# Row maxima of the prompt attention over 128 rows of q, and gate selection over 128 rows

## The chip, the cores and the metric

One core of a Trainium2 chip runs the whole kernel. The metric is device time in microseconds, the median of the runs of one kernel.

## What is computed

The reference is one step of a decoder layer, for a prompt of 512 positions and for 8 sequences of 4 new positions, with the same weights: a combined projection `h = x @ w_in`, four mixers (state space, short convolution, causal pooling, sparse attention), `w_out`, a layer norm, and a feed-forward part (`relu(x @ w_up)^2 @ w_down`) with another layer norm. All of it is in fp32. The change touches the attention of the prompt, of which this is the core:

```python
# selected and window branch; for 512 positions every block is selected, so both are causal softmax attention
s = jnp.einsum('bqgrd,bkgd->bgrqk', q, k).astype(f32) * (HEAD_DIM ** -0.5)
p = jax.nn.softmax(jnp.where(mask, s, NEG_INF), axis=-1)
o = jnp.einsum('bgrqk,bkgd->bqgrd', p, v)
...
gates = jax.nn.sigmoid(g_nsa).reshape(B, T, NSA_HEADS, 3)
y_d = gates[..., 0:1] * o_cmp + gates[..., 1:2] * o_sel + gates[..., 2:3] * o_win
```

There are 8 heads of 64 columns, in 2 groups g of 4 heads r, and 3 branches; the compressed branch works on 8 block averages instead of keys.

## The kernel before, in words

**Precision.** TensorE multiplies in a rounded form of fp32 (float32r). To keep precision, an operand is split into a high part (rounded) and a low part (the rest), and a product is made from three matmuls: high x high, high x low, low x high.

**The main stream.** The projections, `w_out`, `w_up` and `w_down` are a long row of such matmuls: weights of 128x128, activations of 272 columns (half of the 544 positions), into the accumulator `acc`. Weights come by DMA into `raw`; ScalarE makes the high part `wh`, VectorE or GpSimd the low part `wl`.

**Side work.** Everything else is written as Python generators (`gens`). The instruction order of each engine is fixed at build time: a small cost account (`Model`, one clock for each engine) is kept while instructions are written out, and between the matmuls of the main stream `step_side` lets one generator go on, if what it yielded is due: a tile that is ready by the account, a buffer that is free (`FREE_T`, `FREE_S`, `FREE_O`: the PSUM tiles t, s, o), an engine that is not too far behind (`lag`), or a flag. The account prices a float32r matmul by its columns alone unless one side has 32 rows or fewer; 64 and 128 rows cost the same in it. Each engine then runs its list in order, and waits on semaphores where an operand isn't there yet.

**The prompt attention** (`att_prompt`, line 1294) is such side work. There are 16 units u: 2 branches x 4 heads r x 2 groups g. `compressed(r)` makes the compressed branch for each r; `keys_values(br)` brings keys and values: `KH` holds the high part of the keys of g twice, in rows 0 to 63 and 64 to 127; `KL` has 65 rows, the low part of the keys and a row of -1.

**The maxima** (`maxima`, line 1396). For unit u, q is loaded twice into `qraw` (rows 0 to 63 and 64 to 127), and then `q2[:64]` is the high part of q (a copy on ScalarE), `q1` is the high part in all 128 rows (ScalarE), and in `q1[64:]` GpSimd puts the low part (a subtraction of 64x512). So `KH` x `q1`, over 128 rows, is keys-high times q-high plus q-low. The scores for the maxima are computed with the queries as weights, in three groups for each unit: query tiles 0 and 1 (128 and 256 key columns), 2 (384), 3 (512). VectorE masks the diagonal block and takes row maxima; they go by a transpose into row 64 of `q2`, so that the later score matmul (`KL` with `q2`, 65 rows) subtracts them. The maxima need not be exact, as they cancel. Up to NQ = 3 units may be ahead of the values.

**The scores and values.** For each unit and each of 4 key tiles: `KH` x `q1` (128 rows) and `KL` x `q2` (65 rows) into s, the exponential on ScalarE, its split into ph (ScalarE) and pl (GpSimd), three matmuls into o.

**The gates.** `g_done` (line 1276) keeps the sigmoids of the gates in `ghl`: high part in rows 0 to 23, low part in rows 32 to 55, zeros elsewhere. `gate_sel(br, r)` makes a matrix of zeros and ones from `gio`, an iota with the row number within 32 less 12 g: a matmul with it spreads the gate of one branch and head over the 128 rows of the output. It is used 12 times: four in `compressed`, right behind a matmul with the 16 rows of `Vcb`, and eight in `gated`, once for each pair of units.

The lines of the maxima before are 1424 (`yield FREE_T, q2, KL[br, g], ("lag", "V", LM)`) and 1428 (the matmul).

Of the kernel before, what the change touches and what calls it, by code (L numbers as in the profile page):

```python
# [25 lines left out]
F32R = mybir.dt.float32r  # L26
I32 = mybir.dt.int32
# [5 lines left out]
NP, NS, NB, TS = 512, 32, 8, 4  # L33
# [23 lines left out]
LV, LA, LM = 2.5, 2.0, 2.5  # L57
# [155 lines left out]
def tile_hybrid_trunk(ctx: ExitStack, tc: tile.TileContext, x_prompt, x_sample, cache_nsa_kv, cache_win_kv,  # L213
# [8 lines left out]
    V, A, G, PE, SP = (Engine(mdl, e, n) for e, n in ((nc.vector, "V"), (nc.scalar, "A"), (nc.gpsimd, "G"),  # L222
                                                     (nc.tensor, "T"), (nc.sync, "S")))
# [15 lines left out]
    def alloc(pool, tag, shape, dt=F32, bufs=1):  # L239
        t = pool.tile(list(shape), dt, tag=tag, name=nm(tag), bufs=bufs)  # L240
        mdl.alloc(t, tag, bufs)
        return t
# [4 lines left out]
    def ps(tag, shape=(128, 512), bufs=1):  # L247
        return alloc(pside, tag, shape, F32, bufs)

    def psS(shape=(128, 512)):  # L250
        return ps("s", shape, bufs=2)
# [8 lines left out]
    def spawn(gen):  # L260
        gens.append([gen, ()])
# [48 lines left out]
    FREE_T, FREE_O = ("free", "t", 1), ("free", "o", 1)  # L310

    def has(*names):
        return tuple(("flag", n) for n in names)
# [13 lines left out]
    def mm(out, lhsT, rhs, start=True, stop=True):  # L327
        PE.matmul(out, lhsT, rhs, start=start, stop=stop)
# [5 lines left out]
    def halves(t):  # L334
        return t.rearrange("p (h n) -> p h n", h=2)
# [306 lines left out]
    def tp(tag, shape, dt=F32, bufs=1):  # L642
        return alloc(mp, tag, shape, dt, bufs)
# [455 lines left out]
    def cp_tile(n):  # L1099
        return tp("cp", (128, 680), bufs=3)[:, :n]  # L1100
# [105 lines left out]
    KTn = tp("ktn", (128, 2, NS))  # L1206
    Vn = tp("vn", (NS, 2, 128))
    gtok = tp("gtok", (NS, 24))
    ghl = tp("ghl", (64, NP), F32R)
    Kcb, Vcb = tp("kcb", (128, 2, 8)), tp("vcb", (16, 128))  # L1210
    dpool = ctx.enter_context(tc.tile_pool(name="spill", bufs=1, space=bass.MemoryType.DRAM))
    qd = [dpool.tile([128, NP], F32, tag=f"qd{r}", name=nm("qd")) for r in range(4)]
# [63 lines left out]
    def g_done(acc):  # L1276
        gsg = cp_tile(NT)
        A.activation(halves(gsg[:24]), acc[:24, :, :HN], AF.Sigmoid)
        z0 = cp_tile(NP)
        V.memset(z0[:64], 0.0)  # L1280
        V.tensor_copy(ghl, z0[:64])
        A.copy(ghl[0:24, :], gsg[:24, :NP])
        V.tensor_sub(ghl[32:56, :], gsg[:24, :NP], ghl[0:24, :])
        spawn(g_gen(gsg))

    def g_gen(gsg):
        yield gsg, FREE_S
        t = psS()
        tr(t[:NS, :24], gsg[:24, NP:])
        A.copy(gtok, t[:NS, :24])  # L1290
        flags.add("g")


    def att_prompt():
# [4 lines left out]
        def t2(tag, shape, dt=F32, bufs=1):  # L1299
            return alloc(p2, tag, shape, dt, bufs)  # L1300
# [5 lines left out]
        V.tensor_scalar(cmask, ioc, 0.0, None, op0=OP.is_ge)  # L1306
        V.tensor_scalar(kneg, cmask, -1.0, -NEG, op0=OP.add, op1=OP.mult)

        gio = t2("gio", (64, 2, 64), I32)
        for hf in range(2):  # L1310
            G.iota(gio[hf * 32:hf * 32 + 32], pattern=[[-12, 2], [0, 64]], base=0, channel_multiplier=1)

        def gate_sel(br, r):
            gs = t2("gsel", (64, 2, 64), F32R, 2)
            V.tensor_scalar(gs, gio, float(3 * r + br), None, op0=OP.is_equal)
            return gs

# [4 lines left out]
        def compressed(r):  # L1322
# [29 lines left out]
            pT = t2("p", (128, NP))  # L1352
            A.copy(pT[:16], t[:16])
            gs_ = gate_sel(0, r)
            yield pT, gs_, FREE_SS
            op, gp = psS(), psS()
# [11 lines left out]
        KH, KL, VH, VL, Q, G_ = {}, {}, {}, {}, {}, {}  # L1368
# [27 lines left out]
        def maxima():  # L1396


            def load(u):
                r, g = divmod(u % 8, 2)  # L1400
                qr = t2("qraw", (128, NP), bufs=2)
                for dup in range(2):
                    SP.dma_start(qr[dup * 64:dup * 64 + 64], qd[r][g * 64:g * 64 + 64])
                return qr

            nxt = load(0)
            for u in range(16):
                br, g = u // 8, u % 2
                qr = nxt
                if u >= NQ:  # L1410
                    yield has(("pv", u - NQ))
                yield qr,
                q1, q2 = t2("q1", (128, NP), F32R, NQ), t2("q2", (65, NP), F32R, NQ)
                A.copy(q2[:64], qr[:64])
                A.copy(q1, qr)
                G.tensor_sub(q1[64:], qr[64:], q1[64:])
                Q[u] = (q1, q2)
                if u + 1 < 16:
                    nxt = load(u + 1)
                if u % 8 < 2:  # L1420
                    yield has(("kp", br, g))
                mx = t2("mx", (128, 4), bufs=2)
                for qts in ((0, 1), (2,), (3,)):
                    yield FREE_T, q2, KL[br, g], ("lag", "V", LM)
                    s_, c = ps("t"), 0
                    for qt in qts:
                        n = (qt + 1) * 128
                        mm(s_[:, c:c + n], q2[:64, qt * 128:qt * 128 + 128], KH[br, g][:64, :n])
                        c += n
                    c = 0  # L1430
                    for qt in qts:
                        n = (qt + 1) * 128
                        V.tensor_add(s_[:, c + n - 128:c + n], s_[:, c + n - 128:c + n], mask_qk)
                        V.reduce_max(mx[:, qt:qt + 1], s_[:, c:c + n], axis=AX.X)
                        c += n
                yield mx, FREE_T
                mt = ps("t")
                for qt in range(4):
                    PE.transpose(mt[0:1, qt * 128:(qt + 1) * 128], mx[:, qt:qt + 1], ident)
                A.copy(q2[64:65, :], mt[0:1, :])  # L1440
                flags.add(("mx", u))
# [27 lines left out]
        def gated(i, rec, tmp):  # L1469
            br, r = divmod(i, 4)  # L1470
            gs_ = gate_sel(1 + br, r)
            for q in range(4):
                yield rec, LAG_V
                V.reciprocal(rec[:, q * 128:(q + 1) * 128], rec[:, q * 128:(q + 1) * 128])
            yield rec, gs_, FREE_S
            gp = psS()
            mm(gp, gs_.rearrange("p g d -> p (g d)"), ghl)
            V.tensor_mul(rec, rec, gp)
            V.tensor_mul(tmp, tmp, rec)
            V.tensor_add(yd[r][:, :NP], yd[r][:, :NP], tmp)  # L1480
            flags.add(("gated", i))

        yield ("at", mdl.clk["T"] + AT2),
        for r in range(4):
            spawn(compressed(r))
        spawn(keys_values(0))
        gens.insert(0, [maxima(), ()])
        todo = []
        for u in range(16):
            br, g = u // 8, u % 2  # L1490
# [3 lines left out]
            for kt in range(4):  # L1494
# [5 lines left out]
                q1, q2 = Q[u]  # L1500
                s_ = psS()
# [339 lines left out]
    acc = run_tile(U["g"], 0, 24, xr, ks16, True)  # L1841
    drain_side(("kv", KV_ORDER[-1]))
    g_done(acc)
    spawn(att_prompt())
    spawn(att_sample())
    gc_done(0, run_tile(U["gc", 0], 0, 128, xr, ks16, True))
# [424 lines left out]
```

## Time and profile before

| | |
|---|---|
| median of 3 runs | 2464.77 us (2460.89 to 2469.05) |
| profiled execution, its own time | 2462.9 us |
| its span, first to last instruction | 2461.1 us |
| TensorE busy | 2333.4 us, 95% |
| VectorE busy | 1521.9 us, 62% |
| ScalarE busy | 995.8 us, 40% |
| GpSimd busy | 843.9 us, 34% |
| HBM traffic | 107 GB/s over the span |

In the profile PE is TensorE's matmuls, PEld its loads of weights (which run beside matmuls), DVE VectorE, ACT ScalarE, POOL GpSimd and SP the engine that issues DMAs. A matmul counts as busy from its start to a modelled end, so consecutive matmuls overlap, and a busy TensorE may still be slower than it could be: the distance from one start to the next tells more. A row names its output and inputs by the program's tiles: `t<-kh,q` are the matmuls of the maxima, `s<-q,kh` and `s<-q,klm` the scores, `o<-...` the values, `s<-ghl,gsel` the gates, `acc<-...` the main stream. As a helper records every instruction, all have line 160, and one goes by the names.

### The profile page before, as it was taken

Reading aid. Unit: us, or ns where it says so; the run is one execution under the profiler, and the core shown is the slowest. Engines: PE = TensorE matmul, PEld = TensorE weight load, DVE = VectorE, ACT = ScalarE, POOL = GpSimd, SP = SyncE. Lnnn points to the kernel's source line nnn. Section 1 sums busy time; section 2 is a strip of 40 time slices with the busy share of each in tenths; the row PEclk is TensorE's granted clock in tenths of the full one; section 3 lists DMA queues with packets and bytes.
Section 4 is the critical chain, followed back from the end, with each engine's and each line's share of the span. In section 5 each row is a group of like instructions: output and inputs, shape, how many; then the busy total and the mean of one; then the engine's idle time right before and its main releaser. Section 6 shows DMA issues by size and latency. Waiting matters only on the chain. (4 is left out here: it accounts for less than half of the span.)

```text
span 2461.1 us, 46914 instructions
## 1 busy us (share of the span) xinstructions
PE 2333.4 (95%) x18659; PEld 2242.7 (91%) x18659; DVE 1521.9 (62%) x2707; ACT 995.8 (40%) x1941; POOL 843.9 (34%) x726
## 2 busy tenths in 40 slices
PE   7999999998898798999999999999999999999995
PEld 6999888988787687999999999999999999999985
DVE  6873435567544766335694694694694694694256
ACT  3543355554334555323333333333333333333353
POOL 2342245555426598200240240240240240240255
PEclk9999999999999888999999999999999999999998
DMA  6533322322559454422333333233233233233443
GB/s 175 138 91 92 109 69 61 87 66 61 147 154 239 125 138 117 141 86 87 86 90 101 85 90 102 84 90 103 83 91 103 83 90 103 82 91 106 134 155 108
DMA packets 425703, 260.81 MB, mean 106 GB/s; under 512 B 30143, under 2 KB 407067, under 8 KB 425412
## 3 DMA queue, kind: packets, MB, share of 16 engines
q1 hardware_dynamic: 425035, 256.88, 36.6%
q8 instruction: 147, 2.41, 0.4%
q0 software_dynamic: 448, 0.93, 0.2%
q14 instruction: 73, 0.59, 0.1%
HBM read 249.26 MB, written 12.85 MB: 107 GB/s over the span
## 5 line engine op out<-in xcount | busy, mean ns | idle before, releaser
L160 PE MATMUL acc<-B,wh 128*128 128x272 f32 (+1 forms) x3552 | 980.0, 291 | 6.9 <-ACT B L160 2.9
L160 ACT CAST wh<-raw 128x512 fp32r<-128x512 f32 x749 | 462.0, 620 | 826.8 <-PE acc L160 651.9
L160 PEld LDWEIGHTS acc<-B,wh 128*128 128x128 f32 (+1 forms) x3552 | 675.1, 190 | 16.0 <-issue 4.3
L160 PE MATMUL acc<-C,wh 128*128 128x272 f32 x2456 | 676.0, 292 | 13.3 <-DVE C L160 10.0
L160 DVE TENSOR_TENSOR wl<-raw,wh 128x512 fp32r<-128x512 f32 x473 | 407.5, 873 | 326.4 <-ACT wh L160 312.8
L160 PE MATMUL acc<-B,wl 128*128 128x272 f32 x2560 | 580.4, 292 | 0.4 <-POOL wl L160 0.4
L160 POOL TENSOR_TENSOR wl<-raw,wh 128x512 fp32r<-128x512 f32 x276 | 379.1, 1383 | 448.0 <-ACT wh L160 397.9
L160 PEld LDWEIGHTS acc<-C,wh 128*128 128x128 f32 x2456 | 465.7, 191 | 19.7 <-DVE C L160 15.5
L160 PEld LDWEIGHTS acc<-B,wl 128*128 128x128 f32 x2560 | 422.7, 190 | 6.6 <-issue 5.2
L160 PE MATMUL acc<-uh,wh 128*128 128x272 f32 (+2 forms) x1088 | 314.5, 293 | 13.5 <-DVE A L160 13.4
L160 PE MATMUL acc<-ul,wh 128*128 128x272 f32 (+2 forms) x1088 | 309.1, 288 | 0.3 <-DVE fv L160 0.3
L160 POOL TENSOR_TENSOR tt<-raw,raw 128x512 f32<-128x512 f32 x48 | 63.3, 1318 | 714.6 <-DVE S L160 345.2
L160 PE MATMUL acc<-uh,wl 128*128 128x272 f32 (+2 forms) x1088 | 294.4, 290 | 5.6 <-POOL wl L160 5.6
L160 PE MATMUL acc<-A,wh 128*128 128x272 f32 (+1 forms) x992 | 278.9, 299 | 1.2 <-ACT C L160 1.0
L160 PEld LDWEIGHTS acc<-uh,wh 128*128 128x128 f32 x1088 | 206.1, 189 | 21.6 <-issue 17.1
L160 PE MATMUL acc<-A,wl 128*128 128x272 f32 (+1 forms) x992 | 214.0, 297 | 0.6 <-DVE wl L160 0.6
L160 DVE TENSOR_TENSOR A<-A,acc 128x272 f32<-128x272 f32 (+3 forms) x283 | 139.0, 503 | 116.5 <-ACT A L160 79.4
L160 PEld LDWEIGHTS acc<-ul,wh 128*128 128x128 f32 x1088 | 206.5, 190 | 0.6 <-DVE fv L160 0.6
L160 PEld LDWEIGHTS acc<-uh,wl 128*128 128x128 f32 x1088 | 197.6, 189 | 6.9 <-POOL wl L160 6.9
L160 PEld LDWEIGHTS acc<-A,wh 128*128 128x128 f32 (+1 forms) x992 | 187.3, 189 | 8.6 <-issue 4.6
L160 DVE TENSOR_TENSOR wl<-tt,wh 128x512 fp32r<-128x512 f32 x192 | 189.6, 987 | 8.4 <-ACT wh L160 8.4
L160 ACT CAST wh<-tt 128x512 fp32r<-128x512 f32 x192 | 118.6, 621 | 184.3 <-PE acc L160 103.0
(537 smaller groups left out, 3672.4 us busy)
## 6 DMA issues: line engine op xcount, KB each, us to landing
raw<-in_w_up_dram SPq DMA_DIRECT2D x144, 512.0 KB
raw<-in_w_down_dram SPq DMA_DIRECT2D x144, 512.0 KB
raw<-in_w_in_dram SPq DMA_DIRECT2D x52, 512.0 KB
page<-in_cache_nsa_kv_dram SPq DMA_DIRECT2D x64, 256.0 KB
raw<-in_w_out_dram SPq DMA_DIRECT2D x23, 512.0 KB
raw<-in_w_out_dram SPq DMA_DIRECT2D x34, 256.0 KB
C<-in_x_prompt_dram SPq DMA_DIRECT2D x16, 256.0 KB
raw<-in_w_in_dram SPq DMA_DIRECT2D x16, 256.0 KB
```

The costliest lines, as they stand in the source:

```text
L160: r = f(*a, **k)
```

## The change

The matmuls of the maxima use `q1` (128 rows, high and low part of q) and all 128 rows of `KH`, in place of the 64 rows of `q2` and of `KH`; the generator yields `q1` in place of `q2`. For the gates, `ghl`, `gio` and the selection matrices have 128 rows in place of 64: the zeros are written over 128 rows, and the iota runs four times over 32 rows instead of twice. Rows 64 to 127 of `ghl` are zeros, so they add nothing.

```diff
-    ghl = tp("ghl", (64, NP), F32R)
+    ghl = tp("ghl", (128, NP), F32R)
...
-        V.memset(z0[:64], 0.0)
-        V.tensor_copy(ghl, z0[:64])
+        V.memset(z0, 0.0)
+        V.tensor_copy(ghl, z0)
...
-        gio = t2("gio", (64, 2, 64), I32)
-        for hf in range(2):
+        gio = t2("gio", (128, 2, 64), I32)
+        for hf in range(4):
             G.iota(gio[hf * 32:hf * 32 + 32], pattern=[[-12, 2], [0, 64]], base=0, channel_multiplier=1)

         def gate_sel(br, r):
-            gs = t2("gsel", (64, 2, 64), F32R, 2)
+            gs = t2("gsel", (128, 2, 64), F32R, 2)
...
-                    yield FREE_T, q2, KL[br, g], ("lag", "V", LM)
+                    yield FREE_T, q1, KL[br, g], ("lag", "V", LM)
                     s_, c = ps("t"), 0
                     for qt in qts:
                         n = (qt + 1) * 128
-                        mm(s_[:, c:c + n], q2[:64, qt * 128:qt * 128 + 128], KH[br, g][:64, :n])
+                        mm(s_[:, c:c + n], q1[:, qt * 128:qt * 128 + 128], KH[br, g][:, :n])
```

## Rows read from the trace of the kernel before

**Rows 1.** The page: busy us of each engine, share of the span, instructions.
```profile
PE 2333.4 (95%) x18659; PEld 2242.7 (91%) x18659; DVE 1521.9 (62%) x2707; ACT 995.8 (40%) x1941; POOL 843.9 (34%) x726
```

**Rows 2.** Busy time by stretches (columns: PE, PEld, DVE, ACT, POOL, clock, DMA share, GB/s).
```profile
320.00:360.00 40.00, 40.00 (x261) 33.41 (x260) 10.19 (x27) 18.77 (x38) 16.85 (x16) 1.00 0.22 60
...
1040.00:1080.00 40.00, 40.00 (x324) 40.00 (x323) 14.38 (x21) 8.27 (x14) 0.00 (x0) 1.00 0.30 100
```

**Rows 3.** Timeline of TensorE at 337 us: start, duration (us), what, [idle before].
```profile
337.23 0.40 PE L160 MATMUL s<-q,kh 128*128 128x512 f32 x1
337.47 0.39 PE L160 MATMUL s<-q,klm 65*128 65x512 f32 x1
337.70 0.41 PE L160 MATMUL acc<-A,wl 128*128 128x272 f32 x2
```

**Rows 4.** The same at 291 us, unit 1's first group (x2: two matmuls).
```profile
290.74 0.41 PE L160 MATMUL acc<-A,wl 128*128 128x272 f32 x2
291.08 0.49 PE L160 MATMUL t<-kh,q 64*128 64x128 f32 x2
291.50 0.40 PE L160 MATMUL acc<-A,wh 128*128 128x272 f32 x1
291.74 0.29 PE L160 MATMUL acc<-B,wh 128*128 128x272 f32 x1
```

**Rows 5.** The same at 312 us, unit 2's 512-column group.
```profile
311.80 0.29 PE L160 MATMUL acc<-E,wh 128*128 128x272 f32 x1
312.01 0.50 PE L160 MATMUL t<-kh,q 64*128 64x512 f32 x1
312.44 0.52 PE L160 MATMUL acc<-C,wl 128*128 128x272 f32 x2
312.80 0.29 PE L160 MATMUL acc<-A,wh 128*128 128x272 f32 x1
```

**Rows 6.** The same at 426 us, a gate matmul (one acc matmul left out).
```profile
426.16 0.42 PE L160 MATMUL acc<-A,wl 128*128 128x272 f32 x2
426.51 0.50 PE L160 MATMUL s<-ghl,gsel 64*128 64x512 f32 x1
...
427.17 0.29 PE L160 MATMUL acc<-B,wh 128*128 128x272 f32 x1
```

**Rows 7.** The same at 344 us, scores of 128 columns (two rows left out).
```profile
344.01 0.41 PE L160 MATMUL acc<-A,wl 128*128 128x272 f32 x2
344.26 0.22 PE L160 MATMUL s<-q,kh 128*128 128x128 f32 x1
...
344.61 0.29 PE L160 MATMUL acc<-B,wh 128*128 128x272 f32 x1
```

**Rows 8.** Groups of GpSimd, 252 to 640 us: count | busy us, mean ns.
```profile
L160 POOL TENSOR_TENSOR wl<-raw,wh 128x512 fp32r<-128x512 f32 x70 | 93.9, 1344 | 80.4 <-ACT wh L160 68.7 <-PE acc L160 10.2 <-ACT cp L160 1.0
...
L160 POOL IOTA gio<- 32x128 int32 x2 | 0.5, 228 | 0.1
```

**Rows 9.** Weight loads beside kh: ns min/median/max, first and last start (us).
```profile
L160 PEld LDWEIGHTS t<-kh,q x64: 182/183/334, 280.6 to 563.8; 64*128 64x128 f32 x64
...
L160 PEld LDWEIGHTS s<-q,kh x64: 186/188/330, 337.1 to 621.9; 128*128 128x128 f32 x64
```

**Rows 10.** Timeline of GpSimd, unit 1: the subtraction into q1.
```profile
291.56 1.29 POOL L160 TENSOR_TENSOR q<-qraw,q 64x512 fp32r<-64x512 f32 x1 [0.56 <-POOL wl L160]
```

**Rows 11.** Waits of TensorE, 252 to 640 us: total us, times, longest (seven left out).
```profile
PE acc L160 <- DVE C L160: 4.0, 4, 2.0
...
PE s L160 <- ACT p L160: 0.5, 1, 0.5
```

**Rows 12.** Waits of TensorE, 640 to 1000 us, the longest in total.
```profile
PE s L160 <- DMA page<-in_cache_nsa_kv_dram: 10.7, 13, 2.8
```

**Rows 13.** Busy time by stretches around a fall of the clock (columns as in rows 2).
```profile
393.20:403.50 10.30, 9.47 (x34) 7.87 (x33) 8.17 (x14) 2.48 (x6) 4.69 (x4) 0.50 0.29 78
403.50:413.50 10.00, 10.00 (x73) 9.27 (x73) 4.24 (x11) 6.17 (x14) 4.79 (x5) 1.00 0.09 25
```

**Rows 14.** Timeline of TensorE: the last gate matmul of the prompt attention.
```profile
633.93 0.49 PE L160 MATMUL s<-ghl,gsel 64*128 64x512 f32 x1
```

## What the change does to the time: the prediction

> **What bounds the kernel now.** I read the totals first: TensorE is busy for 95% of the span [rows 1]. So the question for any edit is what it does to TensorE's stream. Next I read the busy table by stretches and compared the stretch in which the prompt attention runs as side work (its maxima and gates lie from 280.6 to 633.9 us [rows 9, 14]) with a stretch of the dense part [rows 2]. Both show TensorE busy for 40.00 of 40 us at full clock, yet the first holds 261 matmuls and the second 324. A matmul of 272 columns comes every 0.1235 us in the dense stretch; some of what counts as busy in the attention is therefore time in which TensorE finishes something and feeds nothing. The third view, the timeline of TensorE, shows where that time lies.
>
> The scale is 0.125 us for a 272-column matmul (so 0.46 ns per column); two side matmuls of 512 columns, one with 128 rows and one with 65, follow each other and the stream in 0.47 us, 0.235 each, which is the same scale with nothing over [rows 3].
>
> A group of the maxima with **64 rows** is different. From 290.74 to 291.74 the stream holds two 272-column matmuls, the group's 128 and 256 columns, and one more 272: 3 x 0.125 + 384 x 0.00046 = 0.55 us of columns in 1.00 us. So 0.45 us is lost, part ahead of the group and part behind it: after the matmul at 291.50, the first full-height one, the next starts 0.24 later and not 0.125 [rows 4]. The 512-column group: one 272, the group, two 272 are 0.375 + 0.235 = 0.61 us, and they take from 311.80 to 312.80, so 0.39 us is lost, and no row of it names a wait [rows 5]. The gate matmul (64 rows, 512 columns): two 272, itself and one 272 are 0.61 us and take from 426.16 to 427.17, so 0.40 us is lost [rows 6]. As 65 rows lose nothing and 64 rows lose 0.4 us at the same size, between the same neighbours, I put the loss down to the height of at most 64 rows: at a change between that height and the full one the array seems to be emptied, and the next weights not to be loaded ahead.
>
> Two pages of the Trainium skill pull apart here. "TensorEngine Tiling (Array Packing)", Tiling Modes (Key Properties), says that changing the tiling mode, not only the tile, drains TensorE; it gives no price, and the rows put 0.39 to 0.45 us on one round trip. "TensorE: Matmul & The Clock Gate", in its part on LDWEIGHTS, says that time goes by the columns and that the row count doesn't matter; taken alone it leaves nothing to gain, which is rival (a).
>
> **The change, part by part.** Maxima: 16 units of three groups each (columns 128+256, 384, 512), 64 matmuls. Their row count becomes 128, so they should cost what the 128-row score matmuls beside them cost. Lost today per unit: 0.45 + 0.39 + 0.39 = 1.23 us (for 384 columns I take the value of 512, the nearest row). Left afterwards: nothing for 384 and 512 [rows 3]; for the short one of 128 columns, two such in a row take the stretch from 344.01 to 344.61, which holds three 272 and two 128, 0.375 + 0.118 = 0.49 us, so 0.11 for two and 0.05 for one [rows 7]. Saving 1.23 - 0.06 = 1.17 us per unit, 16 x 1.17 = **18.7 us**. The low bound is half of that, 9 us, if only one of the two sides of a round trip goes; the high bound is 16 x 1.23 = 19.7 us. A loss from streaming itself I exclude, since the same weights and sizes at full height lose nothing [rows 3].
>
> Gates: eight gate matmuls of the two softmax branches stand between full-height matmuls: 8 x 0.40 = 3.2 us. The four of the compressed branch come right behind a matmul of 16 rows (Vcb), so one change of height stays in either case and I count half, 4 x 0.2 = 0.8 us, bounds 0 and 1.6. Together **4.0 us**.
>
> Added work: two more iotas on GpSimd, 2 x 0.23 us, once, before the attention starts [rows 8]; GpSimd is mostly idle there and nobody waits, so nothing; uncovered it would be 0.5 us. The wider memset, copy, and selection tiles have the same elements per partition and so, taken by the durations of before, the same time. The loads of weights take about the same in both heights, 183 and 188 ns in the median [rows 9].
>
> The moved wait: the first group of a unit now waits for all of q1, whose lower half GpSimd writes, and not for q2, which ScalarE writes. In unit 1 that subtraction runs from 291.56 to 292.85 us [rows 10], while the first group ran at 291.08 [rows 4]: 1.77 us too early for the new operand. Behind a waiting matmul on TensorE's queue stands the main stream. If the group kept its place, the price would be up to 16 x 1.77 = 28 us. But the place isn't fixed: the generator yields q1, and the planner emits the group only when its own account has q1 ready, so the group is put about 1.8 us later and main-stream matmuls fill the time. The nearest row is the value matmuls, whose third operand pl is also a GpSimd subtraction and is also waited for in this way: TensorE's list of waits in the attention has nothing of GpSimd among its nine rows [rows 11]. I take 0; bounds 0 and 28. The delay itself hides behind the lead that the maxima have over the scores (up to three units).
>
> Given back: TensorE already waits 13.8 us in this stretch, mostly for VectorE and ScalarE in few places (nine rows, 4.0 to 0.5 us) [rows 11]. A TensorE that is early reaches such a place early and waits longer, by what it saved since the last wait, about 1 us each at the two large places: 2 us. What comes after 640 us (the sample attention, which waits 10.7 us for its pages [rows 12]) starts when the prompt attention ends and shifts with it.
>
> **Sum**: 18.7 + 4.0 - 2 = 20.7 us. The profiled execution took 2462.9 us (its span is 2461.1, with 1.8 us around it), so 2442.2; the median of the runs shown lies 1.9 us above the profiled one, so I forecast **2444 us**.
>
> **Rivals.** (a) The number of rows doesn't matter: the 0.4 us belongs to the place (a write to another PSUM bank, a wait for the copy of q), and stays. Then about 2465. For it: weight loads last the same in both heights [rows 9]. Against: the 65-row matmuls, which also write another bank and also wait for q2 [rows 3]. The second page of the Trainium skill named above (TensorE: Matmul & The Clock Gate, on LDWEIGHTS) speaks for it; [rows 9] agree with it on the load's own duration, and [rows 3 to 5] don't for the stream.
>
> (b) Slower: GpSimd runs behind the planner's account, and the first group of each unit stops the main stream. Place: the subtraction into q1, behind splits of weights on GpSimd of 1.34 us each [rows 8]. The point from which it decides is 22.7 / 16 = 1.42 us of wait per unit; one split ahead eats the gain (16 x 1.34 = 21 us), two cost 16 x 2.69 = 43 us, 2464.8 + 43 - 22.7 = 2485. Against: [rows 11], where nothing waits for GpSimd.
>
> (c) Part is given back behind the attention, or by the new order: the planner's order shifts a little everywhere, and TensorE's clock falls after a pile of waits. A stretch of 10.3 us at half clock held 34 matmuls, the next 10 us at full clock 73 [rows 13]: one such stretch more costs 5 us, and later page loads several more. Two such things leave 8 to 12 us of gain: 2453 to 2460.
>
> (d) More: the stretch at half clock [rows 13] follows waits and contains 64-row groups. If it and the shorter ones go, 5 to 9 us come on top: 2435 and below, to about 2430.
>
> **How the numbers follow.** Forecast 0.66 (2436 to 2453); (a) 0.07; (b) 0.06; (c) 0.12, half of it a gain above the limit; (d) 0.09. Within 0.3%, about what a measurement of this kernel can tell from no change, means 2457.4 to 2472.2. Faster: 0.66 + 0.09 + 0.06 = 0.81; same: 0.07 + 0.06 = 0.13; slower 0.06. The range goes from 2431, into (d), to 2458, into (c); it leaves out (a), (b) and a part of (c) and (d).
>
> **What would show it.** In the profile of after: the maxima's matmuls with 128 rows, about 0.39 us and not 0.5 at 512 columns, and next to them the next stream matmul at its normal distance; more matmuls per 40 us between 280 and 635; the last gate matmul, in the trace of before at 633.93 us [rows 14], about 20 us earlier, and everything behind it shifted by about that much. Wrong step by step: if the distances stay, (a); if waits of TensorE for GpSimd's q1 show up, (b); if the attention ends 20 us earlier and the end of the kernel doesn't, (c).

## The result, and the profile after

| | before | after |
|---|---|---|
| median | 2464.61 us (6 runs, the three above among them) | 2448.33 us (2446.31 to 2451.93, 6 runs) |
| ratio | | 0.9938, 95% interval 0.9926 to 0.9949 |
| profiled execution, span | 2461.1 us | 2446.6 us |
| once more, beside later experiments | 2462.59 us | 2446.03 us, ratio 0.9929 (0.9916 to 0.9942) |

The change takes 16.3 us off the median, 16.6 in the comparison made later; 20.7 were forecast, and 2444 us.

The stretch of [rows 2] in the kernel after, and another of the attention, first before and then after (columns as there):

```profile
320.00:360.00 40.00, 40.00 (x274) 34.78 (x273) 13.31 (x41) 19.18 (x36) 19.14 (x18) 1.00 0.28 75
...
400.00:440.00 40.00, 40.00 (x276) 36.80 (x276) 19.11 (x40) 22.66 (x48) 21.08 (x20) 0.96 0.21 59
400.00:440.00 40.00, 39.92 (x300) 38.27 (x299) 23.12 (x45) 23.15 (x49) 22.75 (x21) 1.00 0.29 80
```

Busy as before, but with 274 matmuls where [rows 2] had 261, and 300 where there were 276 (at a granted clock of 0.96). The timeline of TensorE in the kernel after, for the three forms of [rows 4], [rows 5] and [rows 6]: a group of 128 and 256 columns, one of 512, and a gate.

```profile
357.23 0.29 PE L160 MATMUL acc<-B,wh 128*128 128x272 f32 x1
357.36 0.40 PE L160 MATMUL t<-kh,q 128*128 128x128 f32 x2
357.59 0.41 PE L160 MATMUL acc<-A,wl 128*128 128x272 f32 x2
357.84 0.29 PE L160 MATMUL acc<-A,wh 128*128 128x272 f32 x1
...
323.39 0.29 PE L160 MATMUL acc<-B,wh 128*128 128x272 f32 x1
323.52 0.40 PE L160 MATMUL t<-kh,q 128*128 128x512 f32 x1
323.75 0.41 PE L160 MATMUL acc<-A,wl 128*128 128x272 f32 x2
324.00 0.29 PE L160 MATMUL acc<-A,wh 128*128 128x272 f32 x1
...
413.27 0.41 PE L160 MATMUL acc<-A,wl 128*128 128x272 f32 x2
413.52 0.39 PE L160 MATMUL s<-ghl,gsel 128*128 128x512 f32 x1
413.75 0.29 PE L160 MATMUL acc<-A,wh 128*128 128x272 f32 x1
413.87 0.29 PE L160 MATMUL acc<-B,wh 128*128 128x272 f32 x1
```

The first stretch takes 0.61 us for 0.55 of columns, so 0.06 is lost where 0.45 was; the second 0.61 for 0.61 and the third 0.60 for 0.61, where 0.39 and 0.40 were lost. But not every group looks like this. The waits of TensorE's weight loads between 252 and 640 us (total us, times, longest), first of the kernel before, then of the kernel after, have one line that grew by much:

```profile
PEld t L160 <- DVE mx L160: 1.1, 1, 1.1
```

```profile
PEld t L160 <- DVE mx L160: 4.4, 10, 1.2
```

A group of the maxima waits in ten places for VectorE's row maximum of the group ahead of it, which reads the one PSUM tile t. One of them, on the timeline of weight loads after:

```profile
452.83 0.19 PEld L160 LDWEIGHTS t<-kh,q 128*128 128x128 f32 x1 [0.20 <-DVE mx L160]
```

The matmuls at this place, of which no row names a wait:

```profile
452.43 0.41 PE L160 MATMUL acc<-A,wl 128*128 128x272 f32 x2
452.83 0.50 PE L160 MATMUL t<-kh,q 128*128 128x512 f32 x1
453.17 0.29 PE L160 MATMUL acc<-A,wh 128*128 128x272 f32 x1
```

From 452.43 to 453.17 are 0.74 us for 0.485 of columns, so about 0.25 us of the 0.39 is still lost here.

Two more places matter. The last gate matmul, which stood at 633.93 [rows 14], and the pause of the main stream behind the loop over `op`, where it waits for the sample attention to end (TensorE's timeline; the last matmul of the stream ahead of the pause and the first behind it). Kernel before:

```profile
837.47 0.29 PE L160 MATMUL acc<-B,wl 128*128 128x272 f32 x1
...
867.09 0.60 PE L160 MATMUL acc<-B,wh 128*128 128x272 f32 x1 [0.26 <-ACT B L160]
```

Kernel after:

```profile
628.73 0.39 PE L160 MATMUL s<-ghl,gsel 128*128 128x512 f32 x1
...
814.75 0.37 PE L160 MATMUL acc<-B,wl 128*128 128x272 f32 x1
...
852.24 0.39 PE L160 MATMUL acc<-B,wh 128*128 128x272 f32 x1 [0.26 <-ACT B L160]
```

The stream reaches its pause 22.7 us earlier, 814.75 against 837.47, which is just the sum forecast for the rows, 18.7 and 4.0; but the prompt attention ends only 5.2 us earlier, and the pause lasts 37.5 us and not 29.6. From its end on everything is about as early, 14.9 us there and 14.5 at the end of the span.

### The profile page after: what moved, and what is told of

Its sections match the earlier page's. It is cut to its first block, busy times and chain, and to the rows that moved or that the text cites. A ratio compares the mean times of both kernels' runs of the same rounds, so it can differ in the third digit from the quotient of the medians.

```text
span 2446.6 us, 46935 instructions
## 1 busy us (share of the span) xinstructions
PE 2315.5 (95%) x18659; PEld 2243.8 (92%) x18659; DVE 1523.0 (62%) x2707; ACT 996.4 (41%) x1941; POOL 844.1 (35%) x728
## 5 line engine op out<-in xcount | busy, mean ns | idle before, releaser
L160 PEld LDWEIGHTS acc<-C,wh 128*128 128x128 f32 x2456 | 466.3, 191 | 20.9 <-DVE C L160 16.5
```

The lines of the kernel that those rows point to most:

```text
L160: r = f(*a, **k)
```

## The experiments

Four questions: is it the height of 64 rows; what does the new order do; what does the new wait cost; where are the missing microseconds. As the planner fixes the order of every engine by its account, an experiment can keep an order exactly by giving the account the operands that belong to it, while the engine gets others. Times stand beside those of the kernel before of the same comparison (2463.41, 2463.04 and 2462.59 us for the three sets).

**Order and height apart.** First the new order with the old 64 rows:

```diff
-                    yield FREE_T, q2, KL[br, g], ("lag", "V", LM)
+                    yield FREE_T, q1, KL[br, g], ("lag", "V", LM)
...
-                        mm(s_[:, c:c + n], q2[:64, qt * 128:qt * 128 + 128], KH[br, g][:64, :n])
+                        o_ = s_[:, c:c + n]
+                        nc.tensor.matmul(o_, q2[:64, qt * 128:qt * 128 + 128], KH[br, g][:64, :n], start=True, stop=True)
+                        PE.account("matmul", (o_, q1[:, qt * 128:qt * 128 + 128], KH[br, g][:, :n]), {})
```

> The instructions of before (64 rows everywhere) in exactly the order of after: the planner's account is told of q1, so the groups of the maxima are placed as in after, but the matmuls read q2 and 64 rows. My theory (each change between 64 rows and full height costs TensorE 0.4 us, 22.6 us in all, and the new order by itself costs several us because the prompt attention ends later in the main stream): some 20 to 23 us slower than after, 2468 to 2471 us, that is 3 to 7 us slower than before. Rival (the gain is the order's and rows don't matter): like after, 2448 us. Distances around a 64-row group in the trace by my theory: 0.39 to 0.45 us lost, as before.

Measured: 2463.58 us, ratio 1.0001 (0.9987 to 1.0014). So the order alone is worth nothing, and not the 3 to 7 us that I expected it to cost; against this kernel the rows of after are worth 15 to 18 us (medians of 2448.33 and 2446.03). The last gate (timeline of TensorE):

```profile
645.68 0.50 PE L160 MATMUL s<-ghl,gsel 64*128 64x512 f32 x1
```

It stands at 645.68 us, 11.8 later than in the kernel before: in the new order 126 more matmuls of the main stream (3478 against 3352), 15.7 us of them, come ahead of the prompt attention's end. This is why the attention of after ends only 5.2 us earlier. With the rows of after in the same order it moves from 645.68 to 628.73, by 17.0 us, and the end of the span by as much (2463.7 to 2446.6).

Two executions can differ by a few us through the granted clock alone. As an estimate, I count as lost half of the time for which a trace shows it at 0.50, the level of 1.2 GHz. Up to the last gate this is 12.0 us in new_order_64 and 12.0 in after, so the 17.0 us aren't the clock's; in the kernel before it is 10.2. The order of after with 128 rows was profiled twice more up to this point, in after_again and lead below: last gates at 628.33 and 626.50, with 12.0 and 10.2 us lost. Less these, all three stand within 0.5 us (616.3 to 616.8).

Then the old order with the new 128 rows (the same edit the other way round, `yield ... q2` and the account told of q2, the matmul on q1):

> The instructions of after (128 rows everywhere) in exactly the order of before: the account is told of q2, so a group of the maxima keeps its place, and TensorE really waits for GpSimd's half of q1. Theory: the stream gains 22.6 us, and the first group of 12 of the 16 units stands 0.6 to 1.8 us ahead of the end of that subtraction in the trace of before, 15 us of waits; 2455 to 2460 us, with waits for GpSimd's q in the list of TensorE. If the waits cost nothing: 2442. Rival (rows don't matter): 2465 or, with the waits, 2475 to 2480.

Measured: 2460.09 us, ratio 0.9988 (0.9977 to 0.9999), at the upper end of the 2455 to 2460 that the theory gave. The waits of TensorE from 252 to 640 us:

```profile
PE t L1430 <- POOL q L160: 14.0, 12, 1.7
```

Twelve waits for GpSimd's half of q1, 14.0 us, the longest 1.7: these are the places where [rows 10] stands behind [rows 4]. Had the planner left the groups where they were, most of the gain would have gone.

**The height by one row.** Row 64 of q2 gets a copy like the rows above it, and a second copy of the keys has a zero there, so that the result stays that of 64 rows; order of before, no wait for GpSimd:

```diff
-                A.copy(q2[:64], qr[:64])
+                A.copy(q2[:65], qr[:65])
...
+                nc.scalar.copy(kz[:64], kr[:64])
+                nc.vector.tensor_scalar(kz[64:65], neg1[64:65, :].to_broadcast([1, NP]), 0.0, None, op0=OP.mult)
...
-                        mm(s_[:, c:c + n], q2[:64, qt * 128:qt * 128 + 128], KH[br, g][:64, :n])
+                        nc.tensor.matmul(o_, q2[:65, qt * 128:qt * 128 + 128], KZ[br, g][:65, :n], start=True, stop=True)
```

> One row more: the maxima are those of before, but with 65 rows (row 64 of q2 holds a finite value, row 64 of a second copy of the keys is zero, so the result is that of 64 rows), in exactly the order of before and without any wait for GpSimd; four copies of 64x512 on ScalarE and four of one row on VectorE are added. Theory (what counts is whether more than 64 rows are used): 16 x 1.17 = 18.7 us of stream, all in the old order, so 2446 to 2449 us, though the maxima gain no precision and the gates stay at 64 rows. Rival (cost goes with the number of rows, or 128 of them are needed): 2464 us.

Measured: 2449.56 us, ratio 0.9937 (0.9924 to 0.9950). Its timeline of TensorE:

```profile
369.82 0.29 PE L160 MATMUL acc<-B,wh 128*128 128x272 f32 x1
369.95 0.40 PE L1432 MATMUL t<-kz,q 65*128 65x512 f32 x1
370.19 0.42 PE L160 MATMUL acc<-A,wl 128*128 128x272 f32 x2
370.44 0.29 PE L160 MATMUL acc<-A,wh 128*128 128x272 f32 x1
```

From 369.82 to 370.44 are 0.62 us for 0.61 of columns: one row more, and the 0.39 us of [rows 5] are gone. The height is the cause, and 65 rows do as well as 128. The time is 13.9 us less; 18.7 us of stream and 2446 to 2449 us had been expected. The last gate stands at 621.1 us, 12.8 earlier than before, though by the estimate above 3.4 us more were lost to the clock ahead of it (13.7 against 10.2), so some 16 us are won there at equal clock.

**The gates alone** (the lines of the diff on `ghl`, `z0`, `gio` and `gsel`):

> Only the gates have 128 rows; the order of TensorE is that of before. Theory: 8 x 0.40 + 4 x 0.2 = 4.0 us of stream, all of it ahead of the end of the prompt attention: 2460 to 2461 us, gate matmuls of about 0.39 us in place of 0.50. Rival (rows don't matter): 2464.6, no change in distances.

Measured: 2462.66 us, ratio 0.9992 (0.9983 to 1.0001): not told apart from no change. The distances are as expected; its timeline:

```profile
428.31 0.41 PE L160 MATMUL acc<-A,wl 128*128 128x272 f32 x2
428.56 0.40 PE L160 MATMUL s<-ghl,gsel 128*128 128x512 f32 x1
428.80 0.29 PE L160 MATMUL acc<-A,wh 128*128 128x272 f32 x1
```

0.49 us for 0.485, and eight such savings of 0.4 should show as 3 us. The profiled execution has a loss of this size ahead of the gates, in the stretches at the attention's beginning (columns as in [rows 2]), gates_only and then the kernel before:

```profile
272.60:282.60 10.00, 7.86 (x61) 7.35 (x60) 3.88 (x14) 3.40 (x6) 4.14 (x3) 1.00 0.72 218
282.60:292.60 10.00, 10.00 (x39) 8.73 (x40) 4.33 (x14) 1.14 (x2) 1.26 (x1) 0.50 0.20 53
```

```profile
272.60:282.60 10.00, 9.21 (x72) 8.63 (x71) 4.86 (x14) 3.41 (x6) 4.04 (x3) 1.00 0.78 244
282.60:292.60 10.00, 10.00 (x72) 8.87 (x73) 5.18 (x17) 4.08 (x8) 3.62 (x3) 1.00 0.39 118
```

In gates_only TensorE was idle for 2.1 of 10 us, and the granted clock of the next 10 us is 0.50, the level of 1.2 GHz, with 39 matmuls; before, 0.8 us idle, full clock, and 72 matmuls. From 252.6 to 302.6 us gates_only has 308 matmuls and the kernel before 340, though before's clock falls too in the last ten (0.83). Around the 12 gates the distances lose 3.9 us in all, where they lost 7.4 before, so 3.5 us are saved at the gates; but up to the last gate 13.7 us went to the lower clock, where it had been 10.2, and so this execution reaches it only 0.4 us earlier (633.5 us). In this execution the saving is there, and the clock hides it. Whether the timed runs lost their 3 us in the same way isn't settled.

Both parts without the moved wait (65 rows for the maxima, 128 for the gates, order of before):

> Both parts without the moved wait: maxima of 65 rows (as in rows65), gates of 128 rows, order of before. Theory: what rows65 gained (13.9 us) and the gates' 3.5 to 4 us: 2445 to 2447 us, level with after or up to 3 us faster. Rival (the gates' gain is lost again in waits, as gates_only alone showed only about 1 us): 2449.

Measured: 2446.83 us, ratio 0.9935 (0.9922 to 0.9949). Level with after, as expected; beside rows65 the gates' share is within the intervals.

**The missing microseconds.** In after the planner was made to leave the tile t free for 0.4 us before the next group:

```diff
+                elif x[0] == "free_m":
+                    if mdl.free_at(*x[1:3]) + x[3] > now:
+                        return False
...
-                    yield FREE_T, q1, KL[br, g], ("lag", "V", LM)
+                    yield ("free_m", "t", 1, 0.4), q1, KL[br, g], ("lag", "V", LM)
```

> After, and the planner emits a group of the maxima only when its account has had the PSUM tile t free for 0.4 us. Theory (in after TensorE waits ten times, 4.4 us in all, for VectorE's row maximum of the group ahead, which the emptying of the array used to cover): these waits go, 3 to 5 us less, 2443 to 2446 us; the order changes a little too, worth 2 us either way. Rival (the missing 4 us lie elsewhere): 2448.

Measured: 2458.01 us, ratio 0.9981 (0.9973 to 0.9990), some 10 us slower than after; the profiled execution was the fastest of the twelve, 2452.62 us. The test failed as a test: the order changed, and the waits of TensorE from 252 to 640 us are still there, with others beside them.

```profile
PE t L160 <- DVE mx L160: 3.7, 4, 2.0
PE t L160 <- POOL q L160: 3.4, 2, 1.8
```

So it says nothing on the price of the waits, and only that a new order can cost 10 us. The same margin on the 65-row kernel:

> rows65_gates with the same margin of 0.4 us. Theory: its waits of TensorE for the row maxima are already few (about 2 us), so 0 to 2 us faster than rows65_gates, 2443 to 2446 us; the order changes.

Measured: 2450.15 us, ratio 0.9946 (0.9932 to 0.9960), 3 us more than without it, which the intervals don't tell from nothing; it too says nothing on the price of the waits.

A cleaner way keeps the order of after and takes the work away that is waited for: the 64 additions of the mask ahead of the row maxima, which the account still counts. The maxima then run over the whole diagonal block; they only get larger, and cancel. The kernel after was run beside it.

```diff
-                        V.tensor_add(s_[:, c + n - 128:c + n], s_[:, c + n - 128:c + n], mask_qk)
+                        d_ = s_[:, c + n - 128:c + n]
+                        V.account("tensor_add", (d_, d_, mask_qk), {})
```

> The changed kernel once more, on the chip of the next three, so that they can be compared with it: 2446 to 2450 us.

> After, in exactly its order, without the 64 additions of the mask ahead of the row maxima (19 us of VectorE; the maxima then run over the whole diagonal block and are only larger, which cancels). The account still counts them. Theory (in after the groups of the maxima wait ten times for VectorE, 4.4 us, seven of these 0.2 to 0.26 us, less than the 0.3 us that goes per group): most of these waits go and TensorE gains 3 to 4 us: 2444 to 2446 us, with under 2 us of waits for mx left. Rival (these waits aren't what is missing): level with after.

Measured: 2446.03 us for after and 2444.26 without the additions, ratios 0.9929 (0.9916 to 0.9942) and 0.9922 (0.9910 to 0.9935). Waits of the weight loads from 252 to 640 us and the last gate, first after, then without the additions:

```profile
PEld t L160 <- DVE mx L160: 3.2, 9, 0.9
...
628.33 0.39 PE L160 MATMUL s<-ghl,gsel 128*128 128x512 f32 x1
```

```profile
PEld t L160 <- DVE mx L160: 0.4, 1, 0.4
...
622.22 0.39 PE L160 MATMUL s<-ghl,gsel 128*128 128x512 f32 x1
```

Eight of the nine waits are gone, and the attention ends 6.1 us earlier, in the same order: that is more than the waits themselves (3.2 us), as VectorE has 19 us less to do in this stretch. Of these 6.1 us the median shows 1.8, which the intervals don't tell from nothing.

What is lost at the groups can be added up from the timelines: from the start of the matmul ahead of a group to the start of the second one behind it, less 0.46 ns for each column between. Over the 48 groups of the maxima this is 20.2 us in new_order_64, 5.5 in after, 4.2 in after's second execution and 1.3 without the additions; over the 12 gates it is 5.4, and 1.5 in the other three. All four have one order. So the rows bring 18.6 us at these places in after, 19.9 in its second execution, and 22.8 where the maxima don't wait, which is what had been forecast for the rows alone (22.7). That the waits cost 3 to 4 us at their places is shown; how much of the kernel's time they cost is not. The 65-row kernel without the additions:

> rows65_gates in its order (that of before) without the same 64 additions. There the row maxima are waited for only three times, 1.8 us: 1 to 2 us faster than rows65_gates, 2445 to 2446 us, if these waits are what VectorE costs; level with it if VectorE's queue doesn't matter in this order.

Measured: 2442.72 us, ratio 0.9921 (0.9909 to 0.9934), against 0.9935 (0.9922 to 0.9949) with them in another comparison; the intervals overlap. A stretch of the attention (columns as in [rows 2]), the last gate, and TensorE's waits for the page loads of the sample attention from 605 to 870 us, with the additions and then without:

```profile
352.00:402.00 50.00, 47.40 (x317) 44.40 (x316) 28.60 (x66) 27.89 (x60) 28.66 (x28) 0.90 0.28 75
...
620.11 0.39 PE L160 MATMUL s<-ghl,gsel 128*128 128x512 f32 x1
...
PE s L160 <- DMA page<-in_cache_nsa_kv_dram: 7.9, 13, 1.2
```

```profile
352.00:402.00 50.00, 47.89 (x342) 44.72 (x341) 24.52 (x51) 29.74 (x65) 29.54 (x28) 0.97 0.28 75
...
615.18 0.40 PE L160 MATMUL s<-ghl,gsel 128*128 128x512 f32 x1
...
PE s L160 <- DMA page<-in_cache_nsa_kv_dram: 11.8, 12, 3.7
```

The last gate is 4.9 us earlier without the additions, but that is no more than the clock: up to it 17.1 us were lost with them and 12.0 without, 3.5 of the difference in the stretch shown (0.90 and 0.97 of 50 us). So in this order, with three such waits of 1.8 us in all, nothing of the additions shows at the last gate. The main stream goes on after its pause at 849.3 us in both: what the one is ahead is gone by then, and its waits for pages are 3.9 us longer.

**Is the stream's lead worth anything?** In after, 128 matmuls of the main stream between the attention and the pause were left out, with the order kept:

```diff
-            PE.matmul(acc[:m, h, :b - a], wh, xl_[:, a:b], start=False, stop=False)
+            (skip_low if skip else PE.matmul)(acc[:m, h, :b - a], wh, xl_[:, a:b], start=False, stop=False)
...
+    def skip_low(out, lhsT, rhs, **k):
+        PE.account("matmul", (out, lhsT, rhs), k)
```

> After, in its own order, with 128 matmuls of the main stream left out: the products with the low part of the activations in the 16 tiles of oc, 16 us of stream between the prompt attention and the point at which the main stream has to wait for the side work. It leaves that part of the computation out. Theory (behind 640 us the end of the sample attention, not the stream, sets when the main stream goes on): at most 4 us faster than after, and the pause of the main stream grows from 37 us towards 50. Rival (the stream sets it): 14 to 16 us faster, 2433 us, the pause as long as in after.

Measured: 2447.29 us, ratio 0.9938 (0.9923 to 0.9954): nothing gained. Its timeline around the pause, and its waits for pages (605 to 870 us):

```profile
811.70 0.37 PE L160 MATMUL acc<-B,wl 128*128 128x272 f32 x1
...
850.45 0.60 PE L160 MATMUL acc<-B,wh 128*128 128x272 f32 x1 [0.26 <-ACT B L160]
...
PE s L160 <- DMA page<-in_cache_nsa_kv_dram: 20.3, 19, 5.5
```

16 us of matmuls less bring the pause forward by 3.1 us (814.75 in after) and its end by 1.8. The theory held in the time; its detail, a pause that grows to 50 us, didn't: it is 38.8 us long, and the stream waits on the way, for pages 20.3 us (16.8 in after). It also ran at a lower clock: from 640 to 860 us 0.86 was granted, and 0.90 in after, and between the last gate and the pause 13.7 us were lost in this way and not 6.8. So leaving work out of the stream behind 640 us gains nothing here; the run doesn't tell how much of that is waits and how much the clock.

**A version that beats both.** After without the 64 additions, and the account told of it:

> After without the additions, and the account knows it, so the order of everything behind moves too. By the waits alone 2444 to 2446 us; the runs so far put the effect of a new order at 0 to 10 us, mostly a loss, so 2442 to 2456 us. It tells how much of a saving survives a new plan.

Measured: 2431.55 us, ratio 0.9877 (0.9864 to 0.9891), 14.5 us below after and below all that was expected. The last gate and the pause in TensorE's timeline:

```profile
606.83 0.40 PE L160 MATMUL s<-ghl,gsel 128*128 128x512 f32 x1
...
810.48 0.29 PE L160 MATMUL acc<-B,wl 128*128 128x272 f32 x1
...
835.73 0.39 PE L160 MATMUL acc<-B,wh 128*128 128x272 f32 x1 [0.26 <-ACT B L160]
```

The attention ends 21.9 us earlier than in after and the pause 16.5 us earlier, though the stream arrives at it only 4.3 us earlier. In this order the last gate comes behind 3340 matmuls of the stream, not 3478. The granted clock is higher too, 0.979 over the profiled execution and 0.975 in after. How the 14.5 us are shared between the order, the additions and the clock isn't shown.

## Why the prediction was right

**Mechanism: right, and its price too.** At most 64 rows cost TensorE 0.4 us for each change to that height and back. The distances after (0.06, 0, 0) are those that the row-by-row comparison gave, and added up, where the maxima don't wait, they bring 22.8 us for the 22.7 of the sum. Rival (a) is out by rows65: the weight loads last the same and the time doesn't stay. The Trainium skill says that changing the tiling mode drains TensorE (TensorEngine Tiling (Array Packing), Tiling Modes, Key Properties). The trace agrees, if a height of at most 64 rows counts as another mode, with 0.39 to 0.45 us a round trip. The Trainium skill also says of the load of weights that the row count doesn't matter (TensorE: Matmul & The Clock Gate, LDWEIGHTS). In this case that holds for the load's own duration alone (183 and 188 ns). The stream's lead of 22.7 us at its pause has the size of the forecast 22.7, but part of it is the new order, which by itself gives a lead of 8 us there (829.5 in new_order_64's trace) and takes it back in the pause; it doesn't confirm the sum.

**The moved wait: right.** Taken at 0, and TensorE's list of waits after has no line for GpSimd's q. The outer bound of 28 us was the case of an unmoved place: measured 14.0 us. At that price the kernel is within 0.3% of before (ratio 0.9988), the "same" that I gave to (a), and not the "slower" of (b).

**The term that was mis-sized: what is given back, 2 us.** In the order of after the rows bring 17.0 us at the attention's end and 17.1 at the end of the span, not 20.7. I looked for longer waits where TensorE waited already, in [rows 11]. The new ones stand elsewhere: at the groups themselves, where the emptying of the array had covered a wait of 0.2 us for VectorE. The fair comparison is with new_order_64, the same order with 64 rows:

```profile
PEld t L1431 <- DVE mx L160: 1.4, 5, 0.8
```

With 128 rows the line is 4.4 us in ten places, in after's second execution 3.2 in nine; the additions taken away, these waits go. By the distances added up they take 4.2 us of the rows' 22.8 in after, and 2.9 in its second execution. So about 5.8 us (22.8 - 17.0) are given back at the last gate and not 2, most of it at the groups; the last 1.6 of it in after I can't place. In the medians it is not told apart from noise.

**The signpost that was wrong: the last gate 20 us earlier.** It is 5.2 us earlier. I counted on an order that only shifts a little; it put 126 more matmuls ahead of the attention's end. That this cost nothing (new_order_64) was luck as far as my argument goes. In the order of before the signpost holds: with both parts changed (rows65_gates) the last gate is 13.8 us earlier, and 20.7 at equal clock (17.1 us lost up to it, against 10.2). What was right in that step is that the part behind the attention moves with its end, within one order: 17.0 us at the last gate, 16.7 at the end of the pause (868.9 to 852.2). It isn't so always: of the two 65-row executions above, one is 4.9 us ahead at the last gate and level at the end of the pause. Rival (c) was the right kind of thing at the wrong place.

Open: whether the clock also hides the 3 us of gates_only in the timed runs, why the margin costs 10 us, and what the 14.5 us of the last version are made of.

## What to carry to other kernels

A side matmul's cost is the distance between its neighbours, not its own duration: compare one that loses time with one of the same size beside it that doesn't, and the difference (here 64 against 65 rows) names the cause. Before a few us between two traces are read as an effect, look how long each stood at the lower clock up to the point compared. When a stall of one engine goes, look at which waits it had covered, above all at single buffers handed to and fro with another engine. And where a planner fixes the order, test the instruction and the order apart; a gain in the stream counts only as far as it brings forward what is waited for at the next pause.

## What the runs showed of the hardware

A matmul with 65 rows takes part in the stream like one with 128; with 64 rows it costs 0.39 us more at 512 columns, about 0.1 ahead of its start and 0.3 behind it [rows 5, 6], though the loads of weights last 183 and 188 ns. What differs is when the load starts: in the kernel before, the load for a matmul of the maxima starts together with it (0.00 us ahead, median of 64), in the kernel after 0.12 us ahead. I had not expected that a wait of 0.2 us for another engine can hide in such a stall: in the same order the list has five such waits with it and ten without.
